# Standing the transposes of the probabilities together, and pairing the first layer's adaLN steps

## The chip, the cores and the metric

One Trainium2 chip, one of its cores. The metric is the device time of one execution in microseconds (us). The engines are named as the profile names them: PE is TensorE, PEld its weight loads, DVE is VectorE, ACT is ScalarE, POOL is GpSimd, SP is SyncE, which here issues nearly all DMAs. Engines run side by side, each working through its own queue in the order in which the instructions were placed there; semaphores tie them together.

## The reference, cut to what matters

Two layers over 256 tokens of width 1024, float32. In each layer:

```
mod = silu(c) @ w_mod[l] + b_mod[l]              # 6 parts of 1024: adaLN
sh1, sc1, g1, sh2, sc2, g2 = split(mod, 6)
h = rms_norm(x) * (1 + sc1) + sh1
z = h @ w_in                                     # one projection feeds all branches
o_a = MLA attention, 8 heads   (softmax(q k^T) v, causal)
o_b = MoBA attention, 8 heads  (with 256 tokens: causal in one block)
o_c = Conformer convolution, 31 taps
x = x + g1 * ((gate_a o_a + gate_b o_b + gate_c o_c) @ w_out)
h = rms_norm(x) * (1 + sc2) + sh2
x = x + g2 * (w_down(silu(a) * b)),  [a|b] = causal 3-tap conv(h @ w_up)
```

Softmax needs its probabilities transposed before they can be multiplied by v. The part g1 of the first layer (row 2 of `mod`) is needed only when the mixer's output is added to x.

## The kernel before, in words

All weights stream from HBM in pieces of 128 x 1024 float32 (512 KB) into four buffers named `raw` (`wload`, line 196). ScalarE rounds a piece to fp32r (`whi`, line 219), VectorE makes the remainder (`wlo`, line 221), and each product is three matmuls: activation remainder and head with `whi` (lines 297 and 298), head with `wlo` (line 300). The activations are kept in the same two parts (`hh`, `hl`). Pieces are taken three ahead of their use (`take`, `AHEAD`).

The mixer of a layer is a list of tokens (`STEPS`), worked off by the loop that calls `run[tok[0]]`. QKV, UQ, UK, C, G, O, OC and PR are projections that consume weight pieces; MP and BP prepare queries and keys; MA and BA are the attention groups; V are pieces of the 31-tap convolution on VectorE, R pieces of adaLN done on VectorE. `_spread` places tokens of a kind evenly, by the weights in `UNITS`, between two marks. The order of the tokens is the order in which instructions are traced; a planner of the framework then places them on each engine's queue, by the traced order as priority and by its own estimate of when each one's inputs are ready. So the order on the chip is near that of the tokens, but instructions of several tokens are mixed.

`attn4` does one group of four heads, there are eight such groups (MLA and MoBA, two each per layer). Scores go to PSUM, ScalarE takes the exponential (line 641), VectorE the reciprocals of the sums (line 646), and ScalarE scales the probabilities, eight instructions per group (line 653), in the order of heads and query blocks. Then twelve transposes on TensorE (line 662), four to a PSUM bank of the pool `psa` (five banks), each bank copied by ScalarE when its four are done (line 665), and the products with v (line 674). A bank's four slots stand in the order in which their probabilities are scaled, so the fourth is the last to be ready, or ready with the third.

`mod_part` computes one part of adaLN on TensorE. In one step it loads a 512 KB piece of `w_mod` into a `raw` buffer, and does four matmuls in a 128x32 arrangement (line 395), one for each quarter of the PSUM tile `acc`; the profile shows eight records for them. Eight steps k accumulate; a ninth copies, transposes (line 403) and adds the bias. In the first layer's mixer only part 2 is done in this way: nine tokens M, spread between the marks m0 and m1, each running one step (`step(mods)`). Three other parts are computed with the same function around the norms at the layers' middle and boundary, two steps first (`F1`) and the rest behind.

`tc.issue_after(i)` ties the instructions of a block that run on the engine of `i` to come behind `i` in its queue, with no semaphore.

Of the kernel before, what the change touches and what calls it, by code (L numbers as in the profile page):

```python
# [17 lines left out]
P = 128  # L18
# [46 lines left out]
PARTS = [[(0, r) for r in (2, 3, 4) if (0, r) not in RPARTS], []]  # L65
# [22 lines left out]
def _spread(o, items, first, last):  # L88

    i0, i1 = o.index(first), o.index(last)  # L90
    total = sum(UNITS.get(t[0], 0) for t in o[i0:i1])
    res, done, n = [], 0, 0
    for i, t in enumerate(o):
        res.append(t)
        if i0 <= i < i1:
            done += UNITS.get(t[0], 0)
            while n < len(items) and done >= total * (n + 0.5) / len(items) - 1e-9:
                res.append(items[n])
                n += 1
    return res  # L100


def _order(l):
    o = []
    for w in STEPS[l].split():
        name = w.rstrip("0123456789")
        o.append((name, *(int(d) for d in w[len(name):])))
    o = _spread(o, [("V", j, t, min(31, t + TAPS)) for j in range(4) for t in range(0, 31, TAPS)], ("v", 0), ("v", 1))
    if ("r", 0) in o:
        o = _spread(o, [("R", r, k) for n, r in RPARTS if n == l for k in range(KD)], ("r", 0), ("r", 1))  # L110
    o = _spread(o, [("M",)] * (9 * len(PARTS[l])), ("m", 0), ("m", 1))
    return [t for t in o if t[0].isupper() and not (l == 0 and C0K and t[:2] == ("C", 0))]


CFG = {"order": [_order(0), _order(1)]}


# [33 lines left out]
def trunk_kernel(ctx, tc, xT, crow, ccol, pos, invf, modb_d, cols_d, grow_d, wmh, wmr, wm, win1, wqkv,  # L151
                  wgc, wgab, wuq, wukv, woab, woc, wout, wup, wdn, out):
    nc = tc.nc
    te, ac, ve, gp, sy = nc.tensor, nc.scalar, nc.vector, nc.gpsimd, nc.sync
# [12 lines left out]
    def psa():  # L167
        return psp.tile([P, 512], F32, tag="psa", name=nm("psa"), bufs=5)
# [10 lines left out]
    def operand(shape, tag, name, bufs=1, dtype=F32R):  # L179

        return wk.tile(shape, dtype, tag=tag, name=nm(name), bufs=bufs, align_bytes=LINE)
# [131 lines left out]
    ident = cst.tile([P, P], F32, name="ident")  # L313
# [120 lines left out]
    def mod_parts(*parts):  # L434
        for p in parts:
            yield from mod_part(*p)

    def step(gen, n=1):
        for _ in range(n):
            next(gen, None)  # L440
# [151 lines left out]
    def attn4(qT, kT, v, scale, scq, oth, otl, oslot, apart=False):  # L592
# [15 lines left out]
        for t in s0:  # L608
            n = 2 if apart else 4
# [7 lines left out]
        for i, t in enumerate(s0):  # L617
            n = 2 if apart else 4
# [37 lines left out]
        slots = []  # L656
        for ps, _ in prs:
            slots += [ps[0], ps[1][:, 0:P], ps[1][:, P:S], ps[2], ps[3][:, 0:P], ps[3][:, P:S]]
            while len(slots) >= 4:
                pp = psa()  # L660
                for n in range(4):
                    te.transpose(pp[:, n * P:(n + 1) * P], slots[n], ident)  # L662
                slots = slots[4:]
                pt = operand([P, 512], "pT", "pT", 3, F32)
                ac.activation(pt, pp, AF.Copy)
                pts += [pt[:, n * P:(n + 1) * P] for n in range(4)]
        yield

        o = psa()
# [35 lines left out]
    def layer(l):  # L705
# [128 lines left out]
        mods = mod_parts(*((*p, ()) for p in PARTS[l]))  # L834
# [149 lines left out]
        def moba_attn(g):  # L984
            def part(t, h):
                return t[0][64 * (h % 2):64 * (h % 2) + 64, 2 * g + h // 2, :]

            return attn4(lambda h: part(qTb, h), lambda h: part(kTb, h),
                         lambda h, kb: vb[:, kb, (4 * g + h) * 64:(4 * g + h + 1) * 64], None,
                         [scb[b][:, 4 * g:4 * g + 4] for b in range(NB)], obh, obl, 2 * g, True)  # L990
# [48 lines left out]
        def mla_attn(g):  # L1039
            pair = wk.tile([P, 2, 4, S], F32, tag="qkT", name=nm("qkT"), bufs=2, align_bytes=LINE)  # L1040
            qT, kT = pair[:, 0], pair[:, 1]
            for b in range(NB):
                q3 = qa[b].rearrange("p (h c) -> p h c", h=H)
                for src, dst, sc in ((q3, qT, 1.0), (kfs[b], kT, gk[0:96, :])):
                    pt = psa()
                    for h in range(4):
                        te.transpose(pt[0:96, h * P:(h + 1) * P], src[:, 4 * g + h, :], ident)
                    ac.activation(dst[0:96, :, b * P:(b + 1) * P], pt[0:96, :].rearrange("p (h t) -> p h t", h=4),
                                  AF.Copy, scale=sc)
            yield  # L1050
            yield from attn4(lambda h: qT[0:96, h, :], lambda h: kT[0:96, h, :],
                             lambda h, kb: kvs[kb][:, 4 * g + h, 64:128], 96 ** -0.5, None, oah, oal, 2 * g)
# [111 lines left out]
        def attend(fn, g):  # L1164
            if (fn, g) not in attns:
                attns[fn, g] = fn(g)
            step(attns[fn, g])
# [1 line left out]
        run = {  # L1169
            "KL": latents, "LE": lat_evac, "GLU": glu, "LR": lat_rstd, "LT": lat_T, "QKV": proj_qkv, "UQ": up_q, "UK": up_kv,  # L1170
            "MS": mla_rstd, "MP": mla_prep, "BS": moba_rstd, "BP": moba_prep, "MA": lambda g, p: attend(mla_attn, g), "BA": lambda g, p: attend(moba_attn, g), "C": gate_c, "V": conv,
            "LN": conv_mean, "LS": conv_rstd, "LB": conv_silu, "G": gate_ab, "O": out_ab, "OC": out_c, "PR": project, "M": lambda: step(mods),
        }
        if not CDMA:
            rowgen = silu_row(crow1, "kv", 2)
# [124 lines left out]
    for l in range(L):  # L1300
        layer(l)
# [86 lines left out]
```

## Time and profile before

| | |
|---|---|
| three timed runs | median 915.2 us (914.35 to 915.77) |
| the profiled execution, own time | 912.66 us |
| its span, first to last instruction | 910.5 us |
| mean granted TensorE clock | 0.988 |
| PE busy | 889.1 us (98%) |
| DVE busy | 797.0 us (88%) |
| ACT busy | 554.9 us (61%) |
| DMA | 201.59 MB, mean 221 GB/s |

Busy time counts an engine from the start to the end of each instruction. On TensorE matmuls overlap: the next one starts before the record of the last one ends, so what a matmul costs is read from the distance between starts, not from its duration. Where instructions of one kind stand in a row, a line of the order of time merges them and gives their number.

### The profile page before, as it was taken

Reading aid. Unit: us, or ns where it says so; the run is one execution under the profiler, and the core shown is the slowest. Engines: PE = TensorE matmul, PEld = TensorE weight load, DVE = VectorE, ACT = ScalarE, POOL = GpSimd, SP = SyncE. Lnnn points to the kernel's source line nnn. Section 1 sums busy time; section 2 is a strip of 40 time slices with the busy share of each in tenths; the row PEclk is TensorE's granted clock in tenths of the full one; section 3 lists DMA queues with packets and bytes.
Section 4 is the critical chain, followed back from the end, with each engine's and each line's share of the span. In section 5 each row is a group of like instructions: output and inputs, shape, how many; then the busy total and the mean of one; then the engine's idle time right before and its main releaser. Section 6 shows DMA issues by size and latency. Waiting matters only on the chain.

```text
span 910.5 us, 18569 instructions
## 1 busy us (share of the span) xinstructions
PE 889.1 (98%) x7261; PEld 840.1 (92%) x7261; DVE 797.0 (88%) x1553; ACT 554.9 (61%) x979; POOL 46.2 (5%) x36
## 2 busy tenths in 40 slices
PE   6999999999999999999999999899999999999998
PEld 5988888999997999999989989799999799999998
DVE  6989999999987999999775999898987798777774
ACT  4677598645756655556543776885575565565561
POOL 0010700000000000000000043000000000000000
PEclk9999999999999999999999999899999999999999
DMA  8965535699988889997634564156867677666631
GB/s 312 377 201 200 189 117 186 210 330 337 294 292 285 307 278 326 307 308 233 198 101 129 185 231 139 47 183 209 271 220 258 227 233 227 187 192 199 191 94 47
DMA packets 57976, 201.59 MB, mean 221 GB/s; under 512 B 6944, under 2 KB 8480, under 8 KB 57888
## 3 DMA queue, kind: packets, MB, share of 16 engines
q1 hardware_dynamic: 57888, 200.41, 65.5%
q8 instruction: 57, 0.93, 0.4%
q14 instruction: 31, 0.25, 0.1%
HBM read 199.33 MB, written 1.05 MB: 220 GB/s over the span
## 4 chain that ended last, share of the span: by engine, by line
PE 86%; DVE 6%; ACT 5%; issue 1%; DMA 1%; POOL 0%; SPq 0%; POOLq 0%; DVEq 0%; ACTq 0%
PE psb L297 18%; PE psb L298 17%; PE psb L300 17%; PE psa L297 7%; PE psa L298 7%; PE psa L300 7%; PE psa L395 2%; DVE wlo L221 2%; DVE raw L742 2%; ACT whi L219 1%; PE psa L674 1%; ACT p L641 1%; PE psa L607 1%; PE psa L662 1%; PE psa L291 1%
## 5 line engine op out<-in xcount | busy, mean ns | idle before, releaser
L219 ACT ACTIVATE whi<-raw 128x1024 fp32r<-128x1024 f32 (+2 forms) x286 | 296.3, 1042 | 201.8 <-PE psb L298 108.2
L221 DVE TENSOR_TENSOR wlo<-raw,whi 128x1024 fp32r<-128x1024 f32 (+2 forms) x286 | 339.5, 1192 | 59.7 <-ACT whi L219 52.0
L297 PE MATMUL psb<-hh,whi 128*128 128x256 f32 x1088 | 262.0, 282 | 0.1
L298 PE MATMUL psb<-hl,whi 128*128 128x256 f32 x1088 | 259.4, 280 | 0.0
L297 PEld LDWEIGHTS psb<-hh,whi 128*128 128x128 f32 x1088 | 204.5, 188 | 5.7 <-issue 4.6
L298 PEld LDWEIGHTS psb<-hl,whi 128*128 128x128 f32 x1088 | 204.6, 188 | 0.9 <-DVE e L569 0.8
L300 PE MATMUL psb<-hh,wlo 128*128 128x256 f32 x1088 | 148.5, 278 | 0.0
L300 PEld LDWEIGHTS psb<-hh,wlo 128*128 128x128 f32 x1088 | 135.1, 188 | 1.0 <-issue 1.0
L1066 DVE SCALAR_TENSOR_TENSOR cacc<-upad,cw,cacc 128x256 f32<-128x256 f32 x240 | 105.3, 474 | 0.5
L297 PE MATMUL psa<-mhl,whi 128*128 128x256 f32 x400 | 93.2, 276 | 0.0
L298 PE MATMUL psa<-mhl,whi 128*128 128x256 f32 x400 | 93.0, 277 | 0.0
L1263 DVE SCALAR_TENSOR_TENSOR e<-psb,fw,e 128x255 f32<-128x255 f32 (+1 forms) x176 | 83.4, 475 | 8.1 <-ACT e L1261 7.2
L504 POOL TENSOR_TENSOR rs<-rs,mhalf 128x8 f32<-128x8 f32 (+3 forms) x26 | 44.6, 1729 | 672.8 <-DVE rs L503 672.7
L297 PEld LDWEIGHTS psa<-mhl,whi 128*128 128x128 f32 x400 | 74.9, 188 | 0.1
L298 PEld LDWEIGHTS psa<-mhl,whi 128*128 128x128 f32 x400 | 74.9, 188 | 0.0
L1261 ACT ACTIVATE e<-psb,fb,fw 128x256 f32<-128x256 f32 x88 | 48.6, 552 | 29.4 <-DVE e L1263 25.8
L378 DVE SCALAR_TENSOR_TENSOR raw<-raw,crow 128x1024 f32<-128x1024 f32 x48 | 58.1, 1212 | 2.2 <-DMA raw<-in_wmr 2.2
L300 PE MATMUL psa<-mhl,wlo 128*128 128x256 f32 x400 | 53.5, 276 | 0.0
L300 PEld LDWEIGHTS psa<-mhl,wlo 128*128 128x128 f32 x400 | 49.1, 188 | 0.0
L297 PE MATMUL psb<-whi,hh 128*128 128x416 f32 (+1 forms) x96 | 31.9, 357 | 4.5 <-ACT hh L818 4.4
L1271 ACT ACTIVATE mhl<-e 128x256 fp32r<-128x256 f32 x44 | 18.3, 417 | 29.1 <-DVE e L1269 26.7
L298 PE MATMUL psb<-whi,hl 128*128 128x416 f32 (+1 forms) x96 | 30.7, 351 | 0.2 <-DVE hl L819 0.2
(271 smaller groups left out, 1472.5 us busy)
## 6 DMA issues: line engine op xcount, KB each, us to landing
raw<-in_wup SPq DMA_DIRECT2D x88, 512.0 KB, 4.8
raw<-in_wmr SPq DMA_DIRECT2D x60, 512.0 KB, 5.5
raw<-in_wdn SPq DMA_DIRECT2D x44, 512.0 KB, 4.5
raw<-in_wm SPq DMA_DIRECT2D x32, 512.0 KB, 4.4
raw<-in_wgab SPq DMA_DIRECT2D x32, 512.0 KB, 5.0
raw<-in_wqkv SPq DMA_DIRECT2D x24, 512.0 KB, 4.8
raw<-in_win SPq DMA_DIRECT2D x16, 512.0 KB, 4.6
raw<-in_wgc SPq DMA_DIRECT2D x16, 512.0 KB, 4.2
```

The source lines that it names most:

```text
L219: ac.activation(hi, raw, AF.Copy)
L221: ve.tensor_tensor(lo, raw, hi.bitcast(F32), op=ALU.subtract)
L297: te.matmul(o, p1[0], p1[1], start=start, stop=False)
L298: te.matmul(o, p2[0], p2[1], start=False, stop=False)
L300: te.matmul(o, p3[0], p3[1], start=False, stop=stop)
L378: ve.scalar_tensor_tensor(raw, raw, scale, row, op0=ALU.mult, op1=ALU.mult, accum_out=acc)
L395: te.matmul(acc[32 * c:32 * c + 32, 0:S], cact[:, k:k + 1].to_broadcast([P, 32]), raw[:, c * S:(c + 1) * S], start=(k == 0), stop=(k == KD ...
L504: gp.tensor_tensor(r, r, mhalf[:, :n], op=ALU.pow)
L1066: ve.scalar_tensor_tensor(aj, upad[:, j, t:t + S], cw[:, j * 31 + t:j * 31 + t + 1], aj, op0=ALU.mult, op1=ALU.add)
L1261: ac.activation(t, src, AF.Identity, scale=fw[:, 2, c:c + 1], bias=fb[:, c:c + 1])
L1263: ve.scalar_tensor_tensor(t[:, d:S], src[:, 0:S - d], fw[:, 2 - d, c:c + 1], t[:, d:S], op0=ALU.mult, op1=ALU.add)
L1271: ac.activation(mh, th, AF.Copy)
```

## The change: both edits

In `attn4` the transpose of the fourth slot is issued first, and the other three of the bank are tied behind it. In the list of tokens there are five M in place of nine, and each runs two steps. With the same rule of spreading, the pairs then stand behind C00, C20, G20, G50 and, with the closing step, OC1; before, the nine stood behind MA02, MA12, G00, C30, G20, G31, C31, G70 and OC4.

```diff
-    o = _spread(o, [("M",)] * (9 * len(PARTS[l])), ("m", 0), ("m", 1))
+    o = _spread(o, [("M",)] * (5 * len(PARTS[l])), ("m", 0), ("m", 1))
...
                 pp = psa()
-                for n in range(4):
-                    te.transpose(pp[:, n * P:(n + 1) * P], slots[n], ident)
+
+                tr = te.transpose(pp[:, 3 * P:4 * P], slots[3], ident)
+                with tc.issue_after(tr.ins):
+                    for n in range(3):
+                        te.transpose(pp[:, n * P:(n + 1) * P], slots[n], ident)
                 slots = slots[4:]
...
-            [in `run`]  "M": lambda: step(mods),
+            [in `run`]  "M": lambda: step(mods, 2),
```

## Rows read from the trace of the kernel before

**Rows 1.** The page's part 4: the chain that ended last, shares by engine.
```profile
PE 86%; DVE 6%; ACT 5%; issue 1%; DMA 1%; POOL 0%; SPq 0%; POOLq 0%; DVEq 0%; ACTq 0%
```

**Rows 2.** Window: length, busy (count) of PE, PEld, DVE, ACT, POOL; clock, DMA, GB/s.
```profile
95.00:240.00 145.00, 144.53 (x1195) 131.98 (x1193) 142.84 (x287) 97.92 (x200) 13.75 (x7) 1.00 0.67 231
```

**Rows 3.** Groups by line, PE, 100 to 240 us: count, busy us, mean ns, idle.
```profile
L395 PE MATMUL psa<-raw,cact 128*32 128x256 f32 x64 | 6.3, 391 | 0.0
```

**Rows 4.** Order of time on PE, 178.4 to 179.8 us: start, us, instruction.
```profile
178.76 0.64 PE L395 MATMUL psa<-raw,cact 128*32 128x256 f32 x8
179.33 0.39 PE L297 MATMUL psb<-hh,whi 128*128 128x256 f32 x1
179.55 0.28 PE L298 MATMUL psb<-hl,whi 128*128 128x256 f32 x1
```

**Rows 5.** The same on PE, 270.8 to 272.5 us.
```profile
270.83 0.28 PE L292 MATMUL psa<-mhl,whi 128*128 128x256 f32 x1
270.94 0.28 PE L293 MATMUL psa<-mhl,wlo 128*128 128x256 f32 x1
271.15 1.07 PE L395 MATMUL psa<-raw,cact 128*32 128x256 f32 x16
272.15 0.49 PE L525 MATMUL psb<-ones,e 128*128 128x1 f32 x3
```

**Rows 6.** The same on PE, 144.8 to 148.3 us.
```profile
145.13 0.62 PE L395 MATMUL psa<-raw,cact 128*32 128x256 f32 x2
145.68 0.33 PE L662 MATMUL psa<-ident,p 128*128 128x128 f32 x1
145.94 0.62 PE L395 MATMUL psa<-raw,cact 128*32 128x256 f32 x2
146.49 0.44 PE L662 MATMUL psa<-ident,p 128*128 128x128 f32 x2
146.86 0.62 PE L395 MATMUL psa<-raw,cact 128*32 128x256 f32 x4
147.41 0.39 PE L297 MATMUL psb<-hh,whi 128*128 128x256 f32 x1
```

**Rows 7.** The same on PE, 135.0 to 136.0 us.
```profile
135.06 0.27 PE L662 MATMUL psa<-ident,p 128*128 128x128 f32 x1
135.09 0.37 PE L297 MATMUL psb<-hh,whi 128*128 128x256 f32 x1
135.29 0.28 PE L298 MATMUL psb<-hl,whi 128*128 128x256 f32 x1
135.41 0.50 PE L662 MATMUL psa<-ident,p 128*128 128x128 f32 x3
135.66 0.36 PE L297 MATMUL psb<-hh,whi 128*128 128x256 f32 x1
135.87 0.28 PE L298 MATMUL psb<-hl,whi 128*128 128x256 f32 x1
```

**Rows 8.** Line 662, what its engine waited for: us in total, times.
```profile
  ACT p L653: 1.9, 6
```

**Rows 9.** Order of time on PE, 578.6 to 582.4 us.
```profile
579.07 2.20 PE L662 MATMUL psa<-ident,p 128*128 128x128 f32 x9
581.10 0.27 PE L976 MATMUL psa<-ident,mq 128*128 128x128 f32 x1
```

**Rows 10.** Waits of the DMA queue, 90 to 245 us: total, times, longest.
```profile
SPq L196 <- PE psa L395: 12.5, 5, 6.6
```

**Rows 11.** Groups by line, ACT, 150 to 240 us: busy, mean, idle before and until what.
```profile
L219 ACT ACTIVATE whi<-raw 128x1024 fp32r<-128x1024 f32 x28 | 29.7, 1066 | 33.0 <-PE psb L298 26.1 <-DMA raw<-in_wgab 2.5 <-DMA raw<-in_wgc 2.1
```

**Rows 12.** Order of time on PE, 279.5 to 285.4 us.
```profile
283.00 0.64 PE L395 MATMUL psa<-raw,cact 128*32 128x256 f32 x8
```

**Rows 13.** The same on PE, 585.3 to 586.4 us; in brackets the idle time before.
```profile
585.45 0.93 PE L976 MATMUL psa<-ident,mq 128*128 128x128 f32 x4 [2.94 <-ACT qkTb L977]
```

**Rows 14.** The view of rows 2, from 585.4 to 592.5 us.
```profile
585.40:592.50 7.10, 7.05 (x45) 5.87 (x47) 4.32 (x9) 2.67 (x4) 0.00 (x0) 0.52 0.25 78
```

More of the change, by code (lines that the diff above doesn't have):

```diff
@@ L1171, in layer @@
             "MS": mla_rstd, "MP": mla_prep, "BS": moba_rstd, "BP": moba_prep, "MA": lambda g, p: attend(mla_attn, g), "BA": lambda g, p: attend(moba_attn, g), "C": gate_c, "V": conv,
-            "LN": conv_mean, "LS": conv_rstd, "LB": conv_silu, "G": gate_ab, "O": out_ab, "OC": out_c, "PR": project, "M": lambda: step(mods),
+            "LN": conv_mean, "LS": conv_rstd, "LB": conv_silu, "G": gate_ab, "O": out_ab, "OC": out_c, "PR": project, "M": lambda: step(mods, 2),
         }
```

## The prediction

> **What bounds the kernel now.** I read the chain of waits first. TensorE carries 86% of it, VectorE 6%, ScalarE 5% [rows 1]: what shortens the kernel must shorten TensorE's own queue, and a wait that other work covers is worth nothing. Then the busy time by window, for the stretch of the first layer's mixer in which the adaLN steps run. TensorE is busy for 144.53 of 145.00 us there at a granted clock of 1.00, and VectorE for 142.84 [rows 2]. So TensorE has no hole to fill, and VectorE, with 2.16 us free, is close behind it; a TensorE that becomes faster there meets VectorE soon. Then the groups by line: 64 records of the adaLN matmuls (line 395) stand in this stretch, 8 to a step, so 8 steps of one k each [rows 3]. Last, the order of time on TensorE around the steps and around the transposes. Busy time hides there what the distances between starts show, so every price below is a distance from start to start.
>
> **Part 1: the adaLN steps in pairs.** Before, nine tokens M run one step each (eight k steps and the closing one); after, five tokens run two, the tenth finding the generator at its end. Matmuls, loads and the closing copy, transposes and addition stay the same in number. What goes is four times the way into the 128x32 arrangement and back.
> A step alone: 178.76 to 179.33 is 0.57 us until the next matmul of another kind, and the one behind it comes only at 179.55, 0.22 later [rows 4]. Two steps back to back, at the end of the first layer's projection, take 271.15 to 272.15, 1.00 us, so the second k costs 0.43; they are entered 0.21 us after the matmul ahead, where such matmuls otherwise follow each other in 0.11 (270.83 to 270.94) [rows 5]. So a pair saves 2 x 0.57 - 1.00 = 0.14 inside, 0.10 for one entry and, with 0.22 against 0.11, 0.11 for one exit: 0.35 us. Four pairs: 1.40 us.
> The Trainium skill, "TensorEngine Tiling", section Tiling Modes (Key Properties), says that changing the mode, not the tile alone, drains TensorE; "TensorE: Matmul & The Clock Gate", Part 2, puts the drain at about 128 cycles, 53 ns at 2.4 GHz. As an estimate from these pages a pair would save two drains, 0.11 us, and four 0.43 in place of 1.40. The distances of rows 4 and 5 are larger, and I go by them.
>
> **Part 2: the step that the transposes cut up.** The third step (145.13 us) falls among the transposes of a MoBA group. The planner placed 2 records of it, one transpose, 2 records, two transposes, 4 records: 145.13 to 147.41, 2.28 us [rows 6]. A whole step is 0.57, and three transposes are 0.33 (0.11 each, worked out below), so 1.38 us are paid for two interruptions, 0.69 each. By the order of tokens the second pair comes after C20, two tokens behind the transposes of that group, in place of behind G00; and a bank's transposes stand as one block, so that no single one slips between. Ends: 0 (the pair is cut up as before) and -1.38. I take -1.38, since of the eight steps only this one is cut.
>
> **Part 3: the transposes together.** 96 transposes in 24 banks. Among ordinary matmuls a single one at 135.06 delays the second matmul behind it to 135.29: 0.23, less 0.12 for the matmul between, is 0.11. Three at 135.41 delay it to 135.87: 0.46 less 0.12 is 0.34, again 0.11 each [rows 7]. A transpose pays no way in or out there, and standing together saves nothing. What can change is the waiting. The fourth slot of a bank reads the latest scaled probabilities, so the new first transpose waits longest, and behind it on TensorE, in issue order, waits whatever the planner put there. All transposes together waited 1.9 us for the scaling [rows 8]. Where there was nothing else to run, nine in a row took 579.07 to 581.10, 2.03 us against 9 x 0.11 = 0.99: 1.04 us of trickling [rows 9]. After, the same end is set by the same last scaling, but two or three more transposes stand behind it, 0.22 to 0.33 us, until ScalarE may copy the bank; 24 banks have other matmuls to cover that, except at this place. Ends: -1.9 (all the waiting goes) and +1.04 (a second call trickles uncovered). I take 0, by rows 7, which are the nearest.
>
> **Part 4: loads.** Each step's 512 KB takes one of four raw buffers until TensorE has read it; a pair holds two, and on SP's queue the weight loads stand behind. Five times in this stretch a load waited for such a release, 6.6 us at the longest, 12.5 in all [rows 10]. It is covered: ScalarE's splits, which use the loads, stood idle 33.0 us there, 26.1 of it for TensorE to release a buffer, and only 4.6 for the two kinds of load named [rows 11]. Cost 0; without the cover a late weight unit could cost TensorE up to those 6.6 us once. The accumulator's PSUM bank is taken about one token later and released earlier, which costs nothing.
>
> **The sum.** TensorE: -1.40 - 1.38 + 0 = -2.78 us. VectorE, whose work does not change, has 2.16 us free in the same 145 us [rows 2], so I cut the gain at 2.2. Some of its work (the rows of adaLN, which use the same engine) could go behind this stretch, but in an engine that issues in order I don't count on it. The profiled execution took 912.66 us, its span 910.5 and 2.2 around it: it becomes 910.5. The three timed runs have a median of 915.2, 2.5 above the profiled one; carried there, 915.2 - 2.2 = 913.0.
>
> **The rivals.**
> Pairs come apart (27%). Nothing ties the two halves: each waits for its own load. Where loads are late, steps traced back to back stand alone, as the one at 283.00 does among ordinary matmuls [rows 12]. For it too: VectorE's 2.16 us leave little to win. Against it: the steps of this stretch have their data early, and rows 5 are two steps traced back to back that stayed together. If half the pairs hold and the cut remains, the gain is 0.70: 914.5.
> The second layer's hole closes (12%). At 585.45 TensorE had idled for 2.94 us [rows 13], and 585.40 to 592.50 then ran at a granted clock of 0.52, which is nearly all at the 1.2 GHz level [rows 14]; at 2.4 GHz it would take some 7.1 x 0.52 = 3.7, so 3.4 are lost. The transposes of rows 9 stand just ahead, so moving them can change what the planner puts in the hole: -2.2 - 2.9 - 3.4 = -8.5, 906.7. Against it: what ended the hole is ScalarE's and VectorE's preparation of MoBA's second half, which nothing here moves.
> A new hole (16%), the other side. The first transpose of a bank waits for the latest probabilities, and TensorE can't pass it. Where the step of rows 6 now fills the scaling, 145.13 to 147.41, after the change stands a waiting transpose. If that becomes an idle time like the 2.94 us of rows 13, the clock falls as it did there: the 3.4 us of the lower clock and 2.28 us of uncovered scaling, less 2.2 of gain, is +3.5, 918.7. The point from which it decides is a hole as long as that of rows 13, the one seen here ahead of a lower clock; a shorter one is priced at its own length and leaves 913 to 915. Against it: weight matmuls were ready at 147.41 and can come forward.
> The Trainium skill, "TensorE: Matmul & The Clock Gate", Part 2, speaks for this rival: TensorE pulls weight loads ahead, but matmuls stay in program order, so a matmul that waits for one semaphore stops all behind it. By that rule the change puts the longest wait of each bank in front; the trace of before shows it only as the 1.9 us of rows 8.
>
> **How the numbers follow.** The forecast has 45%, its own range 912.0 to 914.2 (from the full 2.78 with 0.4 of the waiting of part 3, to 1.0 when only three pairs hold). The range of 8 in 10 goes from 908.0, half-way into the closed hole, to 917.5, into the new one. About 0.2%, 1.8 us, is what a measurement of this kernel can tell from no change. Faster by more: three quarters of the forecast's 45%, the 12% and a little of the pairs that come apart, 0.49. Slower: the new hole, mostly, 0.15. Within: 0.36.
>
> **What would show it.** In the order of time, line 395 between 95 and 240 us must stand in four runs of 16 records, each about 1.00 us long, with no transpose inside; runs of 8 show the first rival. Transposes must stand in fours at 0.11 us, as often waiting for the scaling as before. The hole of rows 13 and its lower clock should be as they were, and no new stretch below a clock of 1.00 should stand between 95 and 240. If VectorE bounds, its idle time in that window falls towards zero and TensorE's rises. The prediction is wrong if the planner's other choices, which both edits disturb, move more than the steps do: then the difference will stand outside this window, or on lines that the change doesn't touch.

## The result and the profile after

| | before | after |
|---|---|---|
| median of 6 runs each (us) | 914.88 (912.31 to 916.04) | 920.88 (917.66 to 922.99) |
| ratio, 95% interval | 1 | 1.0057 [1.0035, 1.0078] |
| profiled execution, its span (us) | 912.66, 910.5 | 921.98, 919.9 |
| first scores, norm behind the first layer's mixer, end (us) | 107.7, 272.15, 910.55 | 107.08, 276.65, 919.85 |

The change made the kernel 5 to 6 us slower; I had forecast 2.2 us faster. From the first scores to the norm behind the first layer's mixer it was 164.45 us before and is 169.57 after: the +5.1 us stand in the stretch that the change touches. The rest of the two spans' difference lies behind that norm, where of the change only the second layer's transposes stand: from it to the end the kernel before took 638.4 us and the kernel after 643.2, but 637.0 in a second profile of it (`after_again`, below), with 169.85 us for the stretch ahead of the norm. So the 5 us in the stretch come again, and the rest differs between executions of one kernel; I don't count it to the change.

The chain of waits of the kernel after, for [rows 1]:

```profile
PE 78%; DVE 9%; ACT 7%; DMA 3%; issue 2%; SPq 0%; POOL 0%; POOLq 0%; DVEq 0%; ACTq 0%
```

TensorE has lost 8 points to VectorE, ScalarE and the transfers. By window, with the columns of [rows 2]:

```profile
95.00:240.00 145.00, 138.77 (x1162) 127.24 (x1160) 140.10 (x283) 95.33 (x195) 13.12 (x7) 1.00 0.65 228
```

The clock is 1.00 as before, and 33 matmuls fewer (1162 for 1195) were done in the same time: TensorE was free for 6.2 us where it had been for 0.5. So it isn't the clock, and not the matmuls' own length. VectorE was not the bound either: it too did less, 140.10 us for 142.84. On TensorE, in the order of time, three of four pairs stand as I had drawn them:

```profile
122.78 1.07 PE L395 MATMUL psa<-raw,cact 128*32 128x256 f32 x16
...
179.40 1.07 PE L395 MATMUL psa<-raw,cact 128*32 128x256 f32 x16
180.40 0.39 PE L297 MATMUL psb<-hh,whi 128*128 128x256 f32 x1
```

16 records in 1.00 us, as in [rows 5]. The second pair is cut, and now waits besides (the bracket is the idle time before):

```profile
147.07 0.62 PE L395 MATMUL psa<-raw,cact 128*32 128x256 f32 x2
148.26 0.33 PE L662 MATMUL psa<-ident,p 128*128 128x128 f32 x1 [0.57 <-ACT p L653]
148.43 0.49 PE L665 MATMUL psa<-ident,p 128*128 128x128 f32 x3
148.85 1.06 PE L395 MATMUL psa<-raw,cact 128*32 128x256 f32 x14
149.84 0.48 PE L605 MATMUL psb<-qkTb 64*128 64x128 f32 x2
```

Most of the idle time is elsewhere. Around the third pair the DMA queue of the kernel before and of the one after, in the order of time (first before, then after):

```profile
171.19 0.33 SPq L196 DMA_DIRECT2D raw<-in_wm  x1
172.32 0.33 SPq L196 DMA_DIRECT2D raw<-in_woab  x1
174.64 0.33 SPq L196 DMA_DIRECT2D raw<-in_wgab  x1
176.57 0.33 SPq L196 DMA_DIRECT2D raw<-in_wmr  x1
178.31 1.48 SPq L196 DMA_DIRECT2D raw<-in_wgab  x2
```

```profile
171.75 1.46 SPq L196 DMA_DIRECT2D raw<-in_wm  x2
175.26 0.33 SPq L196 DMA_DIRECT2D raw<-in_woab  x1
177.19 0.33 SPq L196 DMA_DIRECT2D raw<-in_wmr  x1
178.92 1.98 SPq L196 DMA_DIRECT2D raw<-in_wgab  x3
```

`in_wm` is adaLN's piece. Before, it takes one of the four buffers, and the gate's weights (`in_wgab`) are asked for at 174.64; after, two are taken at 171.75 and stay taken until the pair has run at 180.40, the buffers left go to `in_woab` and `in_wmr`, and no `in_wgab` is asked for before 178.92, 4.3 us later. Three are then asked for at once; the first landed at 185.12, after 6.2 us, where the one of 174.64 before had landed after 4.5. What follows on ScalarE and TensorE:

```profile
179.66 1.06 ACT L219 ACTIVATE whi<-raw 128x1024 fp32r<-128x1024 f32 x1 [2.86 <-DVE cacc L1069]
185.23 1.06 ACT L219 ACTIVATE whi<-raw 128x1024 fp32r<-128x1024 f32 x1 [4.50 <-PE psb L298]
186.19 0.58 ACT L1118 ACTIVATE b<-psb 128x512 f32<-128x512 f32 x1
```

```profile
185.05 1.07 PE L300 MATMUL psb<-hh,wlo 128*128 128x256 f32 x8
186.83 0.39 PE L297 MATMUL psb<-oah,whi 128*128 128x256 f32 x1 [0.71 <-ACT b L1118]
```

The profile names VectorE's `cacc` and TensorE's `psb` for the idle time before these splits. The landings say otherwise: the splits of 179.66, 185.23 and 186.93 start 0.10 to 0.11 us after their pieces had landed (179.56, 185.12, 186.82). Line 298's last use of the buffer that the split of 185.23 needs ended at 182.49; before, the same split came 0.04 us behind such an end (181.48, 181.52), its piece having landed at 179.10. So it is 2.7 us late by its load. ScalarE issues in order, so the copy of a PSUM bank (line 1118), which needs nothing of the late piece, stands behind the split, and TensorE waits for the copy. The copy starts at 186.19, 2.8 us after the bank's last matmul ended (183.40); before, the same copy came 0.07 us behind it (182.42, 182.49). VectorE's remainders come late in the same way, and 4 us later two adaLN rows stand ahead of what TensorE needs:

```profile
190.68 1.22 DVE L378 SCALAR_TENSOR_TENSOR raw<-raw,crow 128x1024 f32<-128x1024 f32 x1
191.82 0.08 DVE L378 DVE_READ_ACCUMULATOR raw<-raw,crow 128x1 f32 x1
191.82 0.68 DVE L1129 SCALAR_TENSOR_TENSOR b<-b,psb 128x512 f32<-128x512 f32 x1
```

```profile
192.56 0.39 PE L297 MATMUL psb<-oah,whi 128*128 128x256 f32 x1 [1.34 <-DVE b L1129]
```

More holes stand at 223.38 (0.89 us), 237.96 (0.79) and 240.57 (0.48); these I did not follow back to a load. In all TensorE is idle for 4.81 us between 175 and 245 us, where the kernel before has 0.20. The same place in [rows 11] and after:

```profile
L219 ACT ACTIVATE whi<-raw 128x1024 fp32r<-128x1024 f32 x27 | 28.7, 1066 | 35.5 <-PE psb L298 22.5 <-DVE mod L379 6.3 <-DVE cacc L1069 2.9
```

The idle time in front of the splits grew by only 2.5 us. The sum that I took for cover says nothing of when a wait falls. The queue's own waits, for [rows 10]:

```profile
SPq L196 <- PE psa L395: 22.5, 4, 16.6
```

### The profile page after: what moved, and what is told of

It reads as the page before. It is cut to its first block, busy times and chain, and to the rows that moved or that the text cites. A ratio compares the mean times of both kernels' runs of the same rounds, so it can differ in the third digit from the quotient of the medians.

```text
span 919.9 us, 18568 instructions
## 1 busy us (share of the span) xinstructions
PE 889.5 (97%) x7261; PEld 840.8 (91%) x7261; DVE 798.2 (87%) x1553; ACT 553.3 (60%) x979; POOL 46.2 (5%) x36
## 4 chain that ended last, share of the span: by engine, by line
PE 78%; DVE 9%; ACT 7%; DMA 3%; issue 2%; SPq 0%; POOL 0%; POOLq 0%; DVEq 0%; ACTq 0%
PE psb L297 16%; PE psb L298 16%; PE psb L300 15%; PE psa L297 8%; PE psa L298 8%; PE psa L300 7%; DVE wlo L221 3%; DVE cacc L1069 2%; ACT p L641 2%; PE psa L395 2%; ACT whi L219 2%; DMA raw<-in_wmh 1%; PE psa L291 1%; DVE raw L745 1%; ACT p L653 1%
## 5 line engine op out<-in xcount | busy, mean ns | idle before, releaser
L221 DVE TENSOR_TENSOR wlo<-raw,whi 128x1024 fp32r<-128x1024 f32 (+2 forms) x286 | 340.2, 1195 | 67.6 <-ACT whi L219 59.8
```

The lines of the kernel that those rows point to most:

```text
L221: ve.tensor_tensor(lo, raw, hi.bitcast(F32), op=ALU.subtract)
```

## The experiments

**Theory L**: a pair holds two of the four buffers from its load to its run, so weights come late and TensorE waits. Rivals: the transposes cost it (T); the planner's order on TensorE, disturbed by the pairs or by either edit, costs it (P). "Idle" is TensorE's idle time in a window, length less busy.

**One edit at a time.** `e1_transposes` is the kernel before with only the edit in `attn4`; `e2_pairs` only that of the tokens:

```diff
e2_pairs:
-    o = _spread(o, [("M",)] * (9 * len(PARTS[l])), ("m", 0), ("m", 1))
+    o = _spread(o, [("M",)] * (5 * len(PARTS[l])), ("m", 0), ("m", 1))
...
+  "M": lambda: step(mods, 2),
```

> Only the transposes stand together behind the fourth slot; the adaLN steps are single, as before. Theory L (loads: a pair holds two of the four raw buffers, and SP's queue stands still behind it): no change, ratio 0.998 to 1.002, and no wait of SP's queue near 16 us. Rival T (transposes: the wait of a bank's first transpose stops TensorE): the whole loss is here, ratio 1.004 to 1.008. Rival P (the planner's order, disturbed by either edit): some loss, 1.001 to 1.004, with TensorE idle in the window 175 to 245 us.

> Only the adaLN steps in pairs; the transposes as before. Theory L: the whole loss, ratio 1.004 to 1.008, with one wait of SP's queue of 14 us or more for line 395 between 100 and 125 us. Rival T: a gain, 0.997 to 1.000, since four changes of arrangement are saved. Rival P: a loss of its own, 1.001 to 1.004, smaller than that of both edits together.

Measured: e1 0.9997 [0.9973, 1.0021], 914.16 us; e2 1.0061 [1.0032, 1.0091], 919.6 us. The queue's waits for line 395 and the window 95 to 240, first e1, then e2:

```profile
SPq L196 <- PE psa L395: 12.2, 5, 6.6
...
95.00:240.00 145.00, 142.44 (x1185) 130.01 (x1184) 141.44 (x284) 97.16 (x199) 13.76 (x7) 1.00 0.67 229
```

```profile
SPq L196 <- PE psa L395: 23.9, 3, 18.2
...
95.00:240.00 145.00, 135.89 (x1117) 125.03 (x1116) 134.66 (x272) 89.39 (x186) 17.55 (x7) 0.98 0.62 216
```

The loss comes with the pairs. e1 makes no difference that these runs can tell, though its trace is 1.2 us longer from the first scores to the norm (165.66) and has 1.99 us of idle TensorE between 175 and 245 us: differences of that size the times don't show. Its third step, no longer cut, runs in 0.57 us at 144.98. e2 doesn't measure the cost of the buffers alone: its trace also has a hole of 3.10 us ahead of the first scores, which is the second cost found below.

**Two buffers held without pairs.** `e5_ahead` is the kernel before with single steps, each loading the next step's piece ahead:

```diff
-            for i in range(len(raws), min(KD, k + 1 + MAHEAD)):
+            for i in range(len(raws), min(KD, k + 1 + (MAHEAD if tags else 1))):
```

> The kernel before with single steps and its transposes, but each step's piece is loaded one step ahead, so that two of the four raw buffers are held by adaLN while its matmuls stay where they were. Theory L: slower, ratio 1.003 to 1.008, with SP's queue waiting for line 395 for more than the 12.5 us of before. Rivals T and P: no change, 0.998 to 1.002.

Measured: 1.0061 [1.0035, 1.0088], 921.4 us.

```profile
SPq L196 <- PE psa L395: 14.9, 6, 6.8
...
95.00:240.00 145.00, 137.95 (x1142) 124.59 (x1140) 137.05 (x274) 93.40 (x194) 13.64 (x7) 1.00 0.66 220
```

The same loss, the same kind of holes (185.28, 191.76, 227.12 us), with no pair in the kernel. And the queue's longest wait is 6.8 us here, near the 6.6 of before: the 16.6 us standstill of the kernel after, which had struck me first, isn't needed for the loss. What both have is two buffers held. From the first scores to the norm it takes 169.91 us, and the chain is the one followed above: the copy (line 1115 here) runs at 186.43, behind a split of 185.47, though its bank was full at 182.56. Seven of the eight single steps stand near their places in the kernel before (one is parted, 2 records at 161.52 and 6 at 179.00), so this speaks against rival P too.

**Pairs with buffers of their own.** `e3_own` is the kernel after with adaLN's pieces in two buffers (`lh0`, `lh1`) that lie free for most of this stretch; the four `raw` are left to the weights. `e6_pool` asks for those pieces from GpSimd's queue besides. `e3_again` and `after_again` are second profiles.

```diff
-        mods = mod_parts(*((*p, ()) for p in PARTS[l]))
+        mods = mod_parts(*((*p, ("lh0", "lh1")) for p in PARTS[l]))
...
e6_pool, besides:
-                raws.append(wload(wm[l, r, i], tags[i % len(tags)], 1) if tags else wload(wm[l, r, i]))
+                g = gp if (l, r) in PARTS[l] else sy
+                raws.append(wload(wm[l, r, i], tags[i % len(tags)], 1, g) if tags else wload(wm[l, r, i], eng=g))
```

> The changed kernel, but the pieces of the adaLN steps go into two other buffers (lh0 and lh1, free between the latent projections and the convolution's output), so that the four raw buffers serve the weights alone. Theory L: the loss goes, ratio to before 0.997 to 1.001, the long wait of SP's queue for line 395 is gone and TensorE's idle time between 95 and 245 us falls from about 7 us to below 3. Rival T: the loss stays, 1.004 to 1.008. Rival P: it stays in part, 1.002 to 1.006, since the order on TensorE around the pairs is as in the changed kernel.

> The changed kernel, the pieces of the first layer's adaLN steps in two buffers of their own (lh0, lh1) and issued from GpSimd's queue in place of SP's, so that a load that waits for a pair's matmuls stands in front of no weight load. TensorE's order around the pairs is nearly that of the changed kernel. Theory L in its second form (what costs is SP's queue standing behind the adaLN load, whatever buffer it waits for): ratio to before 0.996 to 1.001, no wait of SP's queue for the adaLN matmuls, TensorE idle below 2 us between 95 and 245. Rival P (TensorE's and VectorE's order, as the planner made it for pairs): the loss stays, 1.003 to 1.007.

> A second profile of e3_own (changed kernel, own buffers, SP's queue). If the 7.8 us that one GpSimd power took in its first profile is an accident of that execution, it takes some 3.3 us here and first scores start near 107.3 us; if it belongs to this kernel, it is there again. TensorE's idle time between 175 and 245 us stays below 1 us in either case.

> A second profile of the changed kernel. Theories L and P both say that the holes of the first profile are not accidents: the 16 us wait of SP's queue near 107 us, and TensorE idle for 4 to 6 us between 175 and 245 us, at the same lines.

Measured: e3 1.0041 [1.0018, 1.0064], e6 1.0035 [1.0014, 1.0057]; the second profiles 916.53 and 916.33 us, one run each. Windows of 175 to 245 us of the kernel before, e3 and after_again:

```profile
175.00:245.00 70.00, 69.80 (x598) 67.15 (x597) 69.28 (x134) 36.88 (x52) 0.87 (x1) 1.00 0.91 315
```

```profile
175.00:245.00 70.00, 69.99 (x601) 68.26 (x600) 69.74 (x129) 37.29 (x53) 0.87 (x1) 1.00 0.86 295
```

```profile
175.00:245.00 70.00, 64.71 (x556) 61.53 (x556) 66.85 (x130) 33.66 (x49) 0.86 (x1) 1.00 0.89 311
```

The holes are gone (0.01 us idle; 5.29 in the second profile of the kernel after), as theory L says. I had expected the queue's long wait to go too; in e3 the queue still stands for up to 19.4 us behind adaLN's pieces, and in this window it costs nothing. In e6 it has no such wait at all, and the time is that of e3. Yet the time did not come back. e3 had a new hole, and the first groups of scores ran at half the clock (0.50 from 109.4 to 116.2 us):

```profile
107.13 0.28 PE L298 MATMUL psb<-hl,whi 128*128 128x256 f32 x1
110.50 1.86 PE L605 MATMUL psa<-qkT 96*128 96x128 f32 x7 [3.10 <-ACT qkT L1051]
```

It leads back to GpSimd. The third of the four powers in this stretch (line 504; the second of those of 128x16, for the norm of the MLA queries) took 3.34 us in the kernels before and after, in e1 and in e5, and 7.8 in e2, both profiles of e3, and e6; VectorE then stood 2.79 us for it in e3. From e2:

```profile
94.24 7.84 POOL L504 TENSOR_TENSOR rs<-rs,mhalf 128x16 f32<-128x16 f32 x1 [0.27 <-DVE rs L503]
```

So two costs were mixed, and the next runs were to separate them.

**Attempts that did not separate them.** `e9_gap` and `e11_after_gap` add a small VectorE reduction for the second block, ahead of that power, to break VectorE's run of instructions: in e3 and in the kernel after. `e12_own_from2` and `e15_own_last` give own buffers only to the pieces from k = 2 or k = 4 on, `e13_pairs_own_from2` is e12 without the edit of the transposes, `e14_single_own` has single steps with own buffers for k = 2 to 5.

```diff
e9, e11:
+            if l == 0 and b == 1:
+                ve.tensor_reduce(small(1, "jk1", 1), kss, axis=AX.X, op=ALU.add)
...
e12, e13 (e15: 4 <= i < 8; e14: 2 <= i < 6):
...
-  wload(wm[l, r, i])
+  wload(wm[l, r, i], *((f"lh{i % 2}", 1) if 2 <= i < 8 else ()))
```

> e3_own (changed kernel, the adaLN pieces in two buffers of their own) with one small VectorE reduction of a [128, 8] tile, whose result nobody reads, behind the second block's sums of the MLA norms: VectorE's unbroken run of two-input instructions, beside which GpSimd's third power took 7.82 us in both profiles of e3_own, gets a break. Theory L+G (the raw buffers cost the changed kernel its holes; e3_own wins these back and pays for them at GpSimd): that power takes below 4 us, the 3.1 us hole at 106 us closes, and the ratio to before is 0.996 to 1.001. Rival P (order): it stays at 1.002 to 1.006, with the same power or with other holes.

> The changed kernel with the small reduction alone. Its GpSimd power took 3.34 us in both profiles, so there is nothing to win there. Both theories: unchanged, ratio to before 1.003 to 1.008, the holes between 175 and 245 us as in the changed kernel.

> The changed kernel; pairs 2 to 4 (k 2 to 7) in two buffers of their own, the first pair in the raw ring. Theory L: as e15, ratio 0.997 to 1.002, TensorE idle below 1.5 us between 175 and 245 us. Theory L+G adds: if GpSimd's third power takes 7.8 us here, 3.1 us of idle TensorE stand before the first scores and the ratio is 1.003 to 1.006 in spite of closed holes. Rival P: 1.003 to 1.007 with holes after 175 us.

> e12 without the edit of the transposes. Since the transposes alone made no difference (ratio 0.9997), both theories: within 0.002 of e12.

> The kernel before, single steps; steps k 2 to 5 load into the two buffers, the others into the raw ring. Theory L: the ring was no bound here, so 0.998 to 1.002, and e15 or e12 are at most 1.4 us faster by the changes of arrangement that pairs save. Theory L+G: 1.003 to 1.006 if GpSimd's third power takes 7.8 us.

> The changed kernel; only the last two pairs (steps k 4 to 7) load into two buffers of their own, the first two into the raw ring as there. Up to about 150 us all queues are those of the changed kernel, so GpSimd's third power should take 3.3 us as there. Theory L: the holes between 175 and 245 us (4.8 and 5.3 us of TensorE idle in two profiles) close to below 1.5 us and the ratio to before falls to 0.998 to 1.002. Rival P: the holes stay, ratio 1.003 to 1.007.

| kernel | ratio to before | idle 175 to 245 us | the power, us |
|---|---|---|---|
| e9 (e3 + reduction) | 1.0035 [1.0012, 1.0058] | 0.06 | 7.89 |
| e11 (after + reduction) | 1.0030 [1.0001, 1.0058] | 3.62 | 6.15 |
| e12 (pairs, own from k = 2) | 1.0035 [1.0001, 1.0070] | 0.02 | 7.83 |
| e13 (the same, old transposes) | 1.0027 [1.0001, 1.0052] | 0.61 | 7.82 |
| e14 (single, own for k = 2 to 5) | 1.0047 [1.0017, 1.0077] | 0.67 | 7.83 |
| e15 (pairs, own from k = 4) | 1.0019 [0.9986, 1.0051] | 0.74 | 7.82 |

Wherever the later pieces have buffers of their own the holes close to 0.74 us or less, and wherever they have, the power is long; the reduction was a miss, it cured nothing and made the power of the kernel after longer. e15 shows which pairs make the holes: the first two still hold `raw` buffers there and the holes are gone, so they come from the pairs that fall among the gates' weights from 175 us on. e14 has the long power with single steps and e2 has it without buffers of their own, so neither is needed for it.

**A miss of design.** `e6b_before_pool` and `e10_single_gap` were to be controls: single steps with own buffers, loads on GpSimd's queue, or with the reduction.

> The kernel before, single steps, with the same two buffers and GpSimd's queue for the adaLN pieces. Theory L: no loss, 0.996 to 1.001, since the 12.5 us that SP's queue waited for line 395 were covered already. Rival P: 0.998 to 1.004, any new order costs a little. Beside e6_pool it gives what the pairs are worth when loads are out of the way: theory L says e6_pool is the faster of the two by 0.5 to 1.5 us.

> The kernel before with single steps, the same two buffers of its own on SP's queue and the same small reduction. Theory L+G: no loss, 0.995 to 1.000, the raw ring is free for weights. Beside e9_gap it says what the pairs are worth: 0.5 to 1.5 us by the four saved changes of arrangement, e9_gap faster. Rival P: 0.999 to 1.004.

Measured: 1.0166 [1.0141, 1.0190] and 1.0161 [1.0130, 1.0192]. The nine single steps reach further down the list than five pairs do, and the last comes behind the convolution's output, which uses `lh0` and `lh1`: TensorE stood 8.0 us at 268.96 (6.9 us at 265.33 in e10). They say nothing on the theories.

**The power taken out.** At last the four powers of 128x16 were left out in three kernels: before, after, and e3. VectorE multiplies by the constant in their place, so these kernels don't compute the norm of the MLA queries and serve for comparing times only.

```diff
-        gp.tensor_tensor(r, r, mhalf[:, :n], op=ALU.pow)
+        (ve if n == 16 else gp).tensor_tensor(r, r, mhalf[:, :n], op=ALU.mult if n == 16 else ALU.pow)
```

> The kernel before with the four powers of 128x16 left out (line 504: VectorE multiplies by the constant in their place, so the MLA queries are not normalised; the smaller powers stay). A control: in the kernel before such a power takes 3.3 us and no engine waits long for it. Both theories: 0.998 to 1.002 of before, PE idle 95-245 us within 1 us of before's 0.5.

> The changed kernel with the same four powers left out. Theory L (a pair holds two of four raw buffers, so weights come late): the holes of 175-245 us stay, 3 to 5 us idle, SP waits once for about 16 us, and the time stays 3 to 6 us above the control, 1.004 to 1.007 of before. Rival (the power is the cause also here): idle under 1.5 us and the time within 1 us of the control.

> The changed kernel with the adaLN pieces of the mixer in buffers of their own (as e3_own), with the same four powers left out. Theory L with the power as the second cost: no hole at 107 us and no half clock at 109-116, no holes at 175-245; the time is the control's less the 1.0 to 1.4 us of the pairs: 0.996 to 1.000 of before, 912 to 915 us. Rival (buffers of their own cost by themselves, or the pairs bring nothing even so): 1.002 to 1.004 as e3_own and its kin.

Measured on one chip, beside the kernel before at 915.36 us: e16 0.9998 [0.9980, 1.0016], 915.37 us; e17 1.0033 [1.0019, 1.0048], 918.82 us; e18 0.9972 [0.9957, 0.9987], 912.84 us. The windows of e16, e17 and e18:

```profile
175.00:245.00 70.00, 68.74 (x586) 65.51 (x585) 68.70 (x133) 35.57 (x51) 1.62 (x1) 1.00 0.91 314
```

```profile
175.00:245.00 70.00, 66.91 (x578) 64.47 (x577) 67.17 (x127) 34.46 (x51) 1.62 (x1) 1.00 0.89 308
```

```profile
175.00:245.00 70.00, 69.65 (x597) 67.67 (x596) 69.56 (x134) 36.82 (x53) 0.87 (x1) 1.00 0.87 300
```

This separates the two. Without the power the changed kernel is still 3.45 us above the control, with its holes (3.09 us idle) and its 17.1 us wait of the queue: the power is no cause of its loss. e17 and e18 differ in their text in nothing but the buffers of adaLN's pieces, and the time falls by 6.0 us, from 918.82 to 912.84; in the two profiles 4.4 us of difference stand between the first scores and the norm. One thing more changes on the chip: with own buffers the planner parts the third pair (16 records at 180.08 in e17; 10 at 160.94 and 6 at 179.13 in e18; in e3 likewise). So these two runs alone don't exclude rival P; against it stand e5, which has such holes and no pair, and the chain from the late load to the wait in the traces of both. With own buffers besides, the holes are gone, the one at 107 us is down to 0.41, and the pairs are 2.5 us below the control: 912.84 to 915.37, the ratio of the two 0.9972 / 0.9998 = 0.997, with an interval of about [0.995, 1.000] from the two half-widths. From the first scores to the norm: 166.07 us in e16, 168.20 in e17, 163.79 in e18. The control has 1.26 us of idle TensorE in this window, more than I had expected, and is no slower than the kernel before.

What stays open is how much of e18's gain is the steps' own. In its trace two of the four pairs run in 1.00 us, at 124.02 and 208.42; the other two stand as 10 and 6 records, one cut by transposes as in the kernel after, one come apart as said. By Part 1 that is 0.7 us. The norm comes 0.9 us earlier than in e16, but no earlier than in the kernel before (272.10 for 272.15); the rest of the 2.5 is behind it, where there are no pairs. e18 leaves work out and is no kernel to use; one with all the work, own buffers and a short power was not run. No kernel with all the work beat the kernel before; e1 and e15 can't be told from it.

## Why the prediction was wrong

**The failed step is Part 4, loads, priced at 0.** "It is covered" rested on 33.0 us of ScalarE's idle time before its splits [rows 11]. The wait that falls on TensorE was sized at nothing, and three things were wrong in that. I counted an idle engine as cover, but what had to be in time was the load, and the resource was the four `raw` buffers: with two held, two are left. I priced the wait that rows 10 show (6.6 us of the queue) as if it were the cost; e5 loses as much as the change with the longest wait at 6.8, and e3 stands 19.4 us for nothing. And a late piece holds up not its own matmuls first, but whatever stands behind its split in ScalarE's and VectorE's order. The price in the kernel after was 4.81 us of holes of up to 1.34 us each, where e17 and e18 put 6.0 us of time on the buffers; my end "without the cover up to 6.6 us once" held it, though not as one late unit, and I took the other end.

**Part 1 held**: three of four pairs run in 1.00 us. The rival "Pairs come apart" did not decide it.

**Part 2 failed**: the second pair is cut by the transposes. From 147.07 to 149.84 are 2.77 us; less four transposes (0.44) and a whole pair (1.00), 1.33 remain, 0.57 of them the wait for the scaling. That is the 1.38 of the third step before, paid again. In e1 the same step stands uncut: where a step falls decides, not the block.

**Part 3 held in its sum** and not for its reason. Transposes stand in fours, here 0.11 us from the first to the second:

```profile
135.73 0.27 PE L662 MATMUL psa<-ident,p 128*128 128x128 f32 x1
135.84 0.49 PE L665 MATMUL psa<-ident,p 128*128 128x128 f32 x3
136.08 0.97 PE L300 MATMUL psb<-hh,wlo 128*128 128x256 f32 x6
```

The wait for the scaling, [rows 8], did grow, as the first transpose's position says, though the view adds up two engines' idle time:

```profile
  ACT p L653: 6.1, 9
```

Of these 6.1 us, 2.4 are TensorE's own idle time and the rest that of its weight loads; the 1.9 us that I took from [rows 8] as an end for Part 3 were the weight loads' alone, so TensorE had nothing to win there. In e1 the sum is 4.9 us in 8, most of it in the second layer, but from the norm at the layers' boundary to the one behind the second layer's mixer it is 251.6 us there and 251.9 before, so it shows no loss. The rival of the new hole named this wait and put 3.5 us on it; the sign was right and the cause was not. The second layer's hole stayed, so that rival fell too, with [rows 13] now as

```profile
593.54 0.63 PE L979 MATMUL psa<-ident,mq 128*128 128x128 f32 x4 [2.35 <-ACT qkTb L980]
```

The lower clock behind it did not stay as I had said: from 593.5 to 600.6 us it is 0.76 where [rows 14] had 0.52, so it was low for about half as long.

**The sum** was not confirmed. In e18, whose weights are not held up, the time is 2.5 us below its control, near my -2.2; but its trace has two whole pairs of four (0.7 us by Part 1), of Part 2's 1.38 us it pays 0.85 again (147.56 to 149.85, less four transposes and a whole pair), and that VectorE's 2.16 free us cut the gain was tested by no run, so the nearness is in part luck. The range's lower end, called half-way into the closed hole, would be 909.9 by my own terms and not 908.0, which decides nothing here. The range ended at 917.5 since I let the one cost that had no row of its own, two buffers less, end at nothing.

## What to carry to other kernels

Before two steps are joined, count what each holds, for how long, and of how many: a stretch at 99.7% of TensorE with four weight buffers had no second buffer to lend. Idle time of an engine in a sum is not cover; look for the next weight that is asked for later, and for what stands behind its preparation in each engine's order. And if undoing the suspected cost doesn't bring the time back, look in the same trace for a second cost before the theory is dropped.

## What had not been expected of the hardware

GpSimd's power of 128x16 took 3.34 us in four kernels, 6.15 in one and 7.82 to 7.89 in all others that have it at that place, and is the same again in a second profile of the same kernel, so it goes with the order of instructions. VectorE's instructions beside it kept their length (1.22 us for a remainder in both). Where it is long, VectorE runs without a break for the first 5 us of it, mostly on instructions with two operands in SBUF, and then waits 2.79 us for its end (e3). The Trainium skill, "SBUF — State Buffer", section "SBUF: two separate sides", says that GpSimd and such a VectorE instruction exclude each other from a shared pair of ports, each for its whole length. The lengthening agrees in its direction, but VectorE runs without a break in the kernel after too, where the power takes 3.34 us, and the reduction that I put in did not help: what tips it stays open.

Loads of 512 KB took longer to land from 178 us on, in both kernels. In the kernel after, the three asked for within 2 us (178.92 to 180.53 us) took 6.2, 6.7 and 7.6 us, where single ones ahead of them (168.00 to 177.19) took 4.1 to 5.1. In the kernel before, single ones 1.3 to 2.3 us apart (180.27, 182.54, 183.87) took 7.3 to 7.4, where those from 167.37 to 176.57 had taken 3.6 to 4.9. So it isn't shown that asking for three at once made them slow; a load that was held back into this stretch also landed later in it.
